# An encoder trunk on one core: the first group's attention heads are split earlier, into the slots of keys that are no longer used

## The chip, the cores and the metric

The kernel runs on one core of a Trainium2 chip. The time is the device time of one execution in microseconds; where one number stands for a kernel it is the median of several executions. The engines are named as in the profile: PE (TensorE, matrix products and transposes), PEld (its weight loads), DVE (VectorE), ACT (ScalarE), POOL (GpSimd) and SP (SyncE, which here only issues DMAs).

## The reference

Two requests, of 512 and 256 tokens, go through two layers with the same weights. All data is float32, the width is 1024.

```python
for i in range(2):
    h = rms_norm(x, norm_mix[i])
    if i == 0:
        x = x + window_attention(h, w_qkv, w_o, sink, band_bias, in_window)
    else:
        x = x + short_conv(h, w_in, conv_w, w_out)
    h = rms_norm(x, norm_mlp[i])
    x = x + square(relu(h @ w_up[i])) @ w_down[i]
    gate = sigmoid(rms_norm(x, norm_ple[i]) @ w_gate[i])
    x = x + (p[i] @ w_proj[i]) * gate
return rms_norm(x, final_norm)
```

The attention has 16 heads of 64 columns in 4 groups; the four heads of a group share one key head and one value head. A query sees the keys that are at most 128 tokens away, a bias for the distance is added, and each head has a learned sink logit that takes part in the softmax's denominator. The heads' outputs go through the output weights `w_o`.

## The kernel before, in words

Everything is held transposed: a tile has 128 columns of the width as partitions and the 768 tokens of both requests side by side. A float32 product is made of three products of rounded parts: each operand is split into a high part, copied by ACT into a rounded type (line 84), and a low part, the rest, subtracted by DVE (line 85). `split` does both. One block of a product is then high × high, high × low and low × high, and a result of 768 tokens is made in two pieces of 512 and 256 tokens that have a bank of PSUM each (`group`, line 140, and `products`). In the attention there is one bank for the 512 piece and one for the 256 piece, so a second result waits until the first has been read out.

The attention (`mixer_attention`) goes over the 4 groups in `attend(g)`, and in each over six blocks of 128 queries, four of the first request and two of the second; a block is called (g, n). A block makes the scores of its four heads on PE (lines 725 and 726; three banks take turns), reduces each with the bias on DVE (line 727), takes exponentials on ACT (747), sums and reciprocals on DVE, scales the probabilities (753, one head on ACT; 755, three on DVE), transposes them on PE (760), splits them (768, 769), multiplies them with the values (770, 771) and writes the sum of both halves into `heads[g]` (773 on ACT, 778 on DVE).

A table `beside` hangs other work behind certain blocks: the queries of later heads (`queries(c)`, 16 heads in 8 pairs), the second half of the keys, the projection of the second layer's extra inputs, and at the end of group 2 the beginning of the output product. `begin_output`, behind block (2, 4), splits the heads of groups 0 and 1 into four tiles each (`aos`; hi parts in slots 16 to 19, lo parts in 24 to 27). `first_output`, behind block (2, 5), loads the first four 128-column blocks of x (`xa`, slots 0 to 3) and adds the products of groups 0 and 1 with `w_o` to them, three matmuls for each of four terms and each of the two pieces, in the order of the list `aos` (lines 793 and 794). `second_output` does the other four with group 2 as well, and `first_head` the rest after the attention.

The slots are 32 tiles of 128 × 768 in SBUF (and ten more later) that are used again and again by number. Slots 0 and 1 hold the doubled high parts of the keys of groups 0 and 1, slots 2 and 3 their low parts; slots 16 to 31 hold the high and low parts of the normalised input, which the query products read to the last pair, behind block (2, 3). A tile given to a used slot waits until the last reader of the one before is done.

Within the attention's loop nobody writes down the order of the instructions: a scheduler orders each engine's instructions when the program is built. It follows the order of the code, and it pulls a later instruction forward where an engine would have nothing to do by its own reckoning and the slots are free. The engines then run their instructions strictly in the order laid down, each waiting for semaphores. SP's queue of DMAs is such an order too.

After the attention, `xs0` and `act0` (lines 1872 and 1873) are lists of slot numbers from which the first layer's MLP takes its places in order, and the last four of `xs0` go to `second_inputs` for the second layer's extra inputs. Later lists are cut out of these two.

Of the kernel before, what the change touches and what calls it, by code (L numbers as in the profile page):

```python
# [11 lines left out]
F32 = mybir.dt.float32  # L12
# [35 lines left out]
def trunk_kernel(ctx: ExitStack, tc: tile.TileContext, a: dict, out: bass.AP):  # L48
# [33 lines left out]
    def split(hi, lo, src):  # L82

        first = act.activation(hi, src, AF.Copy)
        dve.tensor_tensor(lo, src, hi.bitcast(F32), ALU.subtract)
        return first.ins
# [6 lines left out]
    def weight(src, n, raw=None, tag="w"):  # L93

        m = CH if src is None else src.shape[1]
        if raw is None:
            raw = fetch(src)
        pool, bufs = (wp, 2) if tag == "w" else (more, 1)
        hi, lo = (pool.tile([P, CH], F32R, tag=f"{tag}{p}", name=f"{tag}{p}", bufs=bufs) for p in ("hi", "lo"))
        split(hi[:, :m], lo[:, :m], raw[:, :m])  # L100
        return blocks(hi[:, :m], n), blocks(lo[:, :m], n)
# [48 lines left out]
    def slot(i, name, dt=F32R, n=T):  # L150

        return (slots if i < 32 else more).tile([P, n], dt, tag=f"S{i}", name=name)

    def big(name, dt=F32):

        nonlocal turn
        if more is None:
            return tmp.tile([P, T], dt, tag="t", name=name)
        turn += 1
        return tmp.tile([P, T], dt, tag=f"q{turn % 6}", name=name, bufs=1)  # L160

    def terms_of(w, xs, col=0):

        hi, lo = w
        c = slice(col, col + P)
        return [(wh[:, c], wl[:, c], xh, xl) for wh, wl, xh, xl in zip(hi, lo, *xs)]
# [324 lines left out]
    def mixer_attention():  # L491
# [25 lines left out]
        def products(terms):  # L517

            if not split_products:
                ps = psum.tile([P, 1024], F32, tag="mm", name="mm")  # L520
                group(ps, terms)
                yield ps[:, :T], 0, T
                return
            o = 0
            for i, n in enumerate(SEQS):
                ps = psum.tile([P, 512], F32, tag=f"mm{i}", name="mm", bufs=BM)
                group(ps, [(wh, wl, xh[:, o : o + n], xl[:, o : o + n]) for wh, wl, xh, xl in terms], n)
                yield ps[:, :n], o, o + n
                o += n
# [14 lines left out]
        with tc.manual_schedule(engines=order):  # L544
# [21 lines left out]
            hi = wp.tile([P, CH], F32R, name="whi", bufs=2)  # L566
            lo = wp.tile([P, CH], F32R, name="wlo", bufs=2)
# [25 lines left out]
        with s1:  # L593
# [29 lines left out]
            def queries(c):  # L623
                w = wq[0] if c == 0 else weight(a["w_q"][c], KB, raw=wq[1] if c == 1 else None)
                t = big("qt")
                for ps, o, e in products(terms_of(w, xs)):
                    dve.scalar_tensor_tensor(t[:, o:e], ps, HD**-0.5, r[:, o:e], ALU.mult, ALU.mult)
                hi = big("qh", F32R)
                lo = big("ql", F32R)
                split(hi[:], lo[:], t[:])  # L630
                for j in range(2):
                    h = 2 * c + j
                    qst[h] = slot(QS[h % 8], "q")
                    for i, part in enumerate((hi, lo)):
                        nc.sync.dma_start(
                            qst[h][64 * i : 64 * i + 64, :].bitcast(F32),
                            part[64 * j : 64 * j + 64, :].bitcast(F32),
                        )
# [11 lines left out]
            for i, raw in enumerate(rawv):  # L650

                m = min(T, 2 * CH - i * T)
                hi, lo = slot((4, 8, 10)[i], "wvh"), slot((5, 9, 11)[i], "wvl")
# [26 lines left out]
            aos = [], []  # L680
            xa = {}
# [100 lines left out]

            def split_heads(g):
                for i in range(2):
                    hi, lo = (slot(16 + 8 * p + 2 * g + i, "aos") for p in range(2))
                    split(hi[:], lo[:], heads[g][:, i, :])
                    aos[0].append(hi[:])
                    aos[1].append(lo[:])
# [6 lines left out]

            def load_part(m0):
                for m in range(m0, m0 + 4):
                    xa[m] = slot(m, "xa", F32)
                    nc.sync.dma_start(xa[m][:], a["x"][m])

            def first_output():
                load_part(0)
                for j in range(2):
                    w = weight(a["w_o0"][j], 4)
                    for i in range(2):
                        output_part(2 * j + i, w, i * P)

            def second_output():
                split_heads(2)
                load_part(4)  # L810
                for m in range(4, KB):
                    output_part(m, weight(a["w_o1"][m - 4], 6))
# [6 lines left out]
            def projected(n):  # L819
                if n == 0:  # L820
                    projw.append(weight(a["proj"][1, 0], 2))
                for m in range(2 * n, 2 * n + 2):
                    step(1, m, projw[0], part1, "t", False)
# [8 lines left out]
                    for p in range(2):  # L832
                        part1[p].append(ps[p][:, k, :])

            def begin_output():
                for g in range(2):
                    split_heads(g)


            beside = {  # L840
                (0, 5): (inputs1, keys1),
                (1, 4): (lambda: projected(0),),
                (1, 5): (lambda: projected(1),),
                (2, 4): (begin_output,),
                (2, 5): (first_output,),
            }
            for g in range(KV - 1):
                for n in range(2):
                    beside[g, 1 + 2 * n] = (lambda c=2 * g + 2 + n: queries(c),)
            for g in range(KV):  # L850
                attend(g)
            second_output()
            split_heads(3)
        return xa, aos

    xa, aos = mixer_attention()
    psum = ctx.enter_context(tc.tile_pool(name="ps", bufs=8, space=PSUM))
    more = ctx.enter_context(tc.tile_pool(name="more", bufs=1))
# [1010 lines left out]

    xs0 = [*range(32, 42), *range(8, 15), *range(7), *range(16, 20)]
    act0 = [7, *range(20, 24), 28, 29, *range(24, 28), 15, 30, 31]

    rest = xs0[17:] + act0
# [109 lines left out]
```

## Time and profile before

| | |
|---|---|
| timed runs, median (lowest to highest) | 1662.21 us (1659.55 to 1662.38), 3 runs |
| the profiled execution's own time | 1661.51 us |
| its span, first to last instruction | 1659.5 us |
| granted PE clock over the span | 0.996 |
| PE, DVE, ACT busy | 1637.6, 1380.8, 948.5 us |

The profile is of one execution. A row of the timeline has the start in us from the span's start, the duration, the engine, the line, the operation, the tile written and the tiles read, the shape, a count of merged instructions, and in brackets how long the engine stood idle before it and which instruction ended that. Matmuls overlap, so the distance of two starts is the price of one and not its duration. A row of the windows has, for each engine, the busy time in that stretch and the number of instructions.

### The profile page before, as it was taken

How to read it: one execution, taken by the hardware profiler on the slowest of the kernel's cores; microseconds unless marked ns; L12 is line 12 of the kernel's file. 1: busy time of each engine (PE TensorE's matmuls, PEld its weight loads, DVE VectorE, ACT ScalarE, POOL GpSimd, SP SyncE). 2: the span in 40 equal slices, each digit the busy share in tenths (PEclk: the TensorE clock that was granted, in tenths of full speed). 3: DMA queues.
4: the chain of work that ended last, by engine and by line, in shares of the span. 5: the costliest groups of instructions: out<-in, count | busy, mean ns of one | idle time of the engine just before them, and what ended most of it. 6: DMA issues, size and time to landing. Idle time of an engine off the chain costs nothing.

```text
span 1659.5 us, 24297 instructions
## 1 busy us (share of the span) xinstructions
PE 1637.6 (99%) x9414; PEld 1587.3 (96%) x9414; DVE 1380.8 (83%) x2242; ACT 948.5 (57%) x1508; POOL 71.7 (4%) x104
## 2 busy tenths in 40 slices
PE   8999999999999999999999999999999999999997
PEld 7988789999999999999999999999999999999986
DVE  7598888898889889877888777778889888988776
ACT  7377766865556556545654434555555655655554
POOL 0211000000000000000000000000000000000000
PEclk9999999999999999999999999999999999999998
DMA  8755322443233333242312222112333323333222
GB/s 267 199 154 149 87 64 83 121 109 87 83 86 96 96 96 91 71 122 69 98 62 77 76 77 76 64 64 73 87 96 96 95 87 79 90 96 108 69 87 99
DMA packets 55476, 161.11 MB, mean 97 GB/s; under 512 B 7056, under 2 KB 10128, under 8 KB 55360
## 3 DMA queue, kind: packets, MB, share of 16 engines
q1 hardware_dynamic: 45184, 139.89, 26.4%
q0 software_dynamic: 10176, 19.67, 6.7%
q8 instruction: 74, 1.21, 0.3%
q14 instruction: 42, 0.34, 0.1%
HBM read 138.82 MB, written 10.48 MB: 90 GB/s over the span
## 4 chain that ended last, share of the span: by engine, by line
PE 88%; DVE 7%; ACT 4%; issue 1%; DMA 0%; DVEq 0%; SPq 0%; ACTq 0%
PE a L486 33%; PE mm L131 10%; PE mm L140 8%; PE b L486 8%; PE d L486 5%; PE c L486 5%; PE B L486 4%; PE C L486 4%; PE gate L140 3%; PE pt L760 1%; PE p L1096 1%; PE p L1199 1%; PE gate L131 1%; PE O L770 1%; PE O L771 1%
## 5 line engine op out<-in xcount | busy, mean ns | idle before, releaser
L486 PE MATMUL a<-xs,whi 128*128 128x384 f32 x624 | 121.8, 337 | 0.0
L444 ACT ACTIVATE vhi<-wraw 128x512 fp32r<-128x512 f32 x67 | 42.2, 631 | 132.3 <-PE B L486 87.9
L486 PEld LDWEIGHTS a<-xs,whi 128*128 128x128 f32 x624 | 110.0, 188 | 0.2 <-DVE y L1306 0.2
L486 PE MATMUL a<-t,zhi 128*128 128x384 f32 x536 | 109.1, 337 | 0.0
L486 PE MATMUL a<-t,whi 128*128 128x384 f32 x536 | 108.8, 336 | 0.0
L486 PE MATMUL b<-t,zhi 128*128 128x384 f32 x536 | 108.7, 336 | 0.0
L1341 DVE TENSOR_TENSOR x<-x,a 128x384 f32<-128x384 f32 x112 | 62.1, 554 | 55.3 <-PE a L486 55.3
L486 PE MATMUL a<-act,whi 128*128 128x384 f32 x448 | 96.5, 337 | 0.0
L486 PEld LDWEIGHTS a<-t,whi 128*128 128x128 f32 x536 | 94.9, 188 | 0.0
L486 PEld LDWEIGHTS b<-t,zhi 128*128 128x128 f32 x536 | 94.9, 188 | 0.0
L486 PEld LDWEIGHTS a<-t,zhi 128*128 128x128 f32 x536 | 94.8, 188 | 0.0
L464 DVE TENSOR_TENSOR wlo<-wraw,whi 128x1024 fp32r<-128x1024 f32 x70 | 85.2, 1218 | 7.9 <-ACT whi L444 7.9
L444 ACT ACTIVATE whi<-sum 128x1024 fp32r<-128x1024 f32 x67 | 70.6, 1054 | 27.0 <-PE a L486 22.7
L464 DVE TENSOR_TENSOR wlo<-sum,whi 128x1024 fp32r<-128x1024 f32 x67 | 81.8, 1220 | 5.1 <-ACT whi L444 5.1
L1058 ACT ACTIVATE y<-y 128x768 f32<-128x768 f32 x64 | 53.7, 839 | 54.4 <-DVE y L1055 54.3
L464 DVE TENSOR_TENSOR zlo<-sum,zhi 128x1024 fp32r<-128x1024 f32 x67 | 81.5, 1217 | 0.0
L140 PE MATMUL mm<-xs_mix,whi 128*128 128x512 f32 (+1 forms) x320 | 81.0, 341 | 0.0
L486 PEld LDWEIGHTS a<-act,whi 128*128 128x128 f32 x448 | 79.8, 188 | 0.0
L444 ACT ACTIVATE whi<-wraw 128x1024 fp32r<-128x1024 f32 x72 | 75.7, 1051 | 7.0 <-PE C L486 7.0
L444 ACT ACTIVATE zhi<-sum 128x1024 fp32r<-128x1024 f32 x67 | 70.9, 1058 | 11.9 <-DVE sum L420 11.0
L486 PE MATMUL a<-xs,wlo 128*128 128x384 f32 x312 | 67.1, 336 | 0.0
L358 ACT ACTIVATE t<-y 128x768 fp32r<-128x768 f32 x56 | 45.7, 838 | 34.9 <-DVE y L349 34.4
(345 smaller groups left out, 4558.4 us busy)
## 6 DMA issues: line engine op xcount, KB each, us to landing
wraw<-in_up SPq DMA_DIRECT2D x64, 512.0 KB, 3.9
wraw<-in_down SPq DMA_DIRECT2D x64, 512.0 KB, 4.2
wraw<-in_w_in SPq DMA_DIRECT2D x24, 512.0 KB, 3.5
wraw<-in_gate SPq DMA_DIRECT2D x16, 512.0 KB, 3.4
vlo<-in_up POOLq DMA_DIRECT2D x28, 256.0 KB, 5.6
vlo<-in_down POOLq DMA_DIRECT2D x28, 256.0 KB, 6.0
pj<-pjs SPq DMA_DIRECT2D x16, 384.0 KB, 2.8
wraw<-in_w_q SPq DMA_DIRECT2D x8, 512.0 KB, 4.6
```

Of the source, the lines that this page charges most:

```text
L131: pe.matmul(t, lhsT=w, rhs=x[:, o:e], start=first and i == 0 and j == 0, stop=last and i == n - 1 and j == 2)
L140: pe.matmul(ps[:, o:e], lhsT=w, rhs=x[:, o:e], start=i == 0 and j == 0, stop=i == n - 1 and j == 2,)
L358: act.activation(t[0][:], (self.q1, self.q2)[i][:], AF.Copy)
L444: act.activation(hi[:], src, AF.Copy)
L464: dve.tensor_tensor(lo[:], src, hi[:].bitcast(F32), ALU.subtract)
L486: pe.matmul(ps, lhsT=a, rhs=b, start=start and i == 0, stop=i == len(terms) - 1, skip_group_check=True)
L760: pe.transpose(pt[:, h * P : (h + 1) * P], lg[h // 2][:, h % 2, b * P : (b + 1) * P], ident[:],)
L770: pe.matmul(O[:], lhsT=v, rhs=ph[:], start=b == 0, stop=False)
L771: pe.matmul(O[:], lhsT=v, rhs=pl[:], start=False, stop=b == nk - 1)
L1058: act.activation(t[:], t[:], AF.Square)
L1096: pe.matmul(ps[o], lhsT=wt[:, c], rhs=xs[f"x{h + 1}{1 + o}"][m][part], start=k == 0 and j == 0, stop=k == KB - 1 and j == 2,)
L1341: dve.tensor_tensor(t[:, o : o + H], t[:, o : o + H], f, op)
```

## The change

The split of group 0's heads is hung behind block (2, 1) instead of (2, 4), and its four tiles go into slots 0 to 3 (hi in 0 and 1, lo in 2 and 3), whose keys are not read after group 1. The split of group 1 stays behind (2, 4). The first four `xa` tiles go into slots 24, 25, 16 and 17 instead of 0 to 3. In `xs0`, slots 0 to 3 move to the end, where the second layer's extra inputs take their places, and 16 to 19 move ahead of them.

```diff
             def split_heads(g):
                 for i in range(2):
-                    hi, lo = (slot(16 + 8 * p + 2 * g + i, "aos") for p in range(2))
+                    hi, lo = (slot(2 * p + i if g == 0 else 16 + 8 * p + 2 * g + i, "aos") for p in range(2))
...
                 for m in range(m0, m0 + 4):
-                    xa[m] = slot(m, "xa", F32)
+                    xa[m] = slot((24, 25, 16, 17, 4, 5, 6, 7)[m], "xa", F32)
                     nc.sync.dma_start(xa[m][:], a["x"][m])
...
-            def begin_output():
-                for g in range(2):
-                    split_heads(g)
...
-                (2, 4): (begin_output,),
+                (2, 4): (lambda: split_heads(1),),
...
+            beside[2, 1] += (lambda: split_heads(0),)
...
-    xs0 = [*range(32, 42), *range(8, 15), *range(7), *range(16, 20)]
+    xs0 = [*range(32, 42), *range(8, 15), *range(4, 7), *range(16, 20), *range(4)]
```

What the scheduler makes of it is seen in the order of the instructions. The first place is DVE at the end of group 2, about 197 to 207 us in the profile of before. `aos` of heads_772 is group 0, of heads_1400 group 1; the numbers behind L, S and O tell buffers apart. Before:

```order
L727 ISA L_2450,mx_2440<-S_2455,bias_1406,sink_77 128x256
L727 ISA mx_2440 128x1
L778 TENSOR_TENSOR heads_2021<-O_2344,ot_2367 64x2x128 x2
L740 TENSOR_SCALAR nm_2459<-mx_2440 128x4
L742 TENSOR_TENSOR es_2461<-sink_77,mx_2440 128x4
L85 TENSOR_TENSOR aos_2507<-heads_772,aos_2506 128x768
L85 TENSOR_TENSOR aos_2511<-heads_1400,aos_2510 128x768
L85 TENSOR_TENSOR aos_2515<-heads_1400,aos_2514 128x768
L748 TENSOR_TENSOR sm_2464<-sm_2464,es_2461 128x4
L727 ISA L_2519,mx_2518<-S_2520,bias_1401,sink_77 128x256
```

And in the changed kernel:

```order
L727 ISA L_2458,mx_2448<-S_2463,bias_1406,sink_77 128x256
L727 ISA mx_2448 128x1
L85 TENSOR_TENSOR aos_2515<-heads_1400,aos_2514 128x768
L778 TENSOR_TENSOR heads_2021<-O_2352,ot_2375 64x2x128 x2
L740 TENSOR_SCALAR nm_2467<-mx_2448 128x4
L742 TENSOR_TENSOR es_2469<-sink_77,mx_2448 128x4
L727 ISA L_2519,mx_2518<-S_2520,bias_1401,sink_77 128x256
L727 ISA mx_2518 128x1
L727 ISA L_2519,mx_2518<-S_2524,bias_1401,sink_77 128x256
```

The three subtractions in one piece are one here, the last of group 1 (its first stands some rows earlier), and the reductions of the next block follow directly.

The second place is PE at the same time. In the changed kernel this stands there, where `mm_2594` and `mm_2608` are the two pieces of the first output block, `aos_2515` the last split of group 1, `mm_2622` the first piece of the second output block, which has the same bank as `mm_2594`:

```order
L140 MATMUL mm_2594<-aos_2515,whi_2590 128x512
L140 MATMUL mm_2594<-aos_2514,wlo_2591 128x512
L140 MATMUL mm_2608<-aos_2515,whi_2590 128x256
L140 MATMUL mm_2608<-aos_2514,wlo_2591 128x256
L725 MATMUL S_2533<-khh_1388,q_1816 128x256
L726 MATMUL S_2533<-kll_1389,q_1816 128x256
L725 MATMUL S_2715<-khh_1394,q_2230 128x256
L726 MATMUL S_2715<-kll_1395,q_2230 128x256
L725 MATMUL S_2719<-khh_1394,q_2233 128x256
L726 MATMUL S_2719<-kll_1395,q_2233 128x256
L725 MATMUL S_2724<-khh_1394,q_2442 128x256
L726 MATMUL S_2724<-kll_1395,q_2442 128x256
```

The next row is the first matmul of `mm_2622`. Before, the last three of these score pairs stood behind the first output block's products with the transposes between, and the order there was this, with `aos_2507` the second split (the low part) of group 0:

```order
L725 MATMUL S_2520<-khh_1388,q_1609 128x256
L726 MATMUL S_2520<-kll_1389,q_1609 128x256
L725 MATMUL S_2524<-khh_1388,q_1612 128x256
L726 MATMUL S_2524<-kll_1389,q_1612 128x256
L725 MATMUL S_2529<-khh_1388,q_1813 128x256
L726 MATMUL S_2529<-kll_1389,q_1813 128x256
L140 MATMUL mm_2594<-aos_2507,whi_2590 128x512
```

The third place is DVE near 169 us, in group 2's first blocks, as a piece of the difference:

```order
-L85 TENSOR_TENSOR wlo<-wraw,whi 128x1024
-L748 TENSOR_TENSOR sm<-sm,es 128x4
-L740 TENSOR_SCALAR nm<-mx 128x4
-L742 TENSOR_TENSOR es<-sink,mx 128x4
-L749 RECIPROCAL sm<-sm 128x4
+L85 TENSOR_TENSOR aos<-heads,aos 128x768
+L748 TENSOR_TENSOR sm<-sm,es 128x4
+L740 TENSOR_SCALAR nm<-mx 128x4
+L742 TENSOR_TENSOR es<-sink,mx 128x4
+L749 RECIPROCAL sm<-sm 128x4
+L85 TENSOR_TENSOR wlo<-wraw,whi 128x1024
 L755 TENSOR_SCALAR L<-L,sm 128x256 x3
```

The second subtraction of group 0 takes the place of that of a query weight, which moves behind the reciprocal and ahead of the scalings. The first one stands near 127 us, behind three scalings; the two copies of ACT stand near 123 and 162 us. On SP the loads of `xa` 0 to 3, which were issued at 108 and 156 us, stand together behind the q loads of the seventh pair of heads and a load of `w_o`, and ahead of the q loads of the eighth pair. From the end of the attention on, the order on every engine is as it was.

## Prediction

> **What bounds the kernel now.** I read the page first: busy shares, then the chain that ended last.
>
> ```profile
> PE 1637.6 (99%) x9414; PEld 1587.3 (96%) x9414; DVE 1380.8 (83%) x2242; ACT 948.5 (57%) x1508; POOL 71.7 (4%) x104
> ...
> PE 88%; DVE 7%; ACT 4%; issue 1%; DMA 0%; DVEq 0%; SPq 0%; ACTq 0%
> ```
>
> TensorE (PE) is the bound nearly everywhere, so an edit pays only where PE stands still or is slow. The next view is the busy time by stretches of 10 us, then of 1 us, around the change. Columns are PE, PEld, DVE, ACT, POOL busy, then the granted clock, the DMA share and GB/s.
>
> ```profile
> 200.00:210.00 10.00, 8.44 (x43) 7.08 (x42) 8.76 (x28) 4.27 (x14) 0.00 (x0) 0.83 0.47 158
> ```
> ```profile
> 201.00:202.00 1.00, 0.00 (x0) 0.00 (x0) 0.97 (x4) 0.47 (x2) 0.00 (x0) 1.00 0.66 169
> 202.00:203.00 1.00, 0.52 (x1) 0.50 (x2) 1.00 (x2) 1.00 (x6) 0.00 (x0) 0.62 1.05 399
> 203.00:204.00 1.00, 1.00 (x4) 0.73 (x3) 1.00 (x2) 0.70 (x4) 0.00 (x0) 0.50 0.55 218
> ```
>
> This is the poorest stretch of the attention stage: PE does nothing from 201 to 202 while DVE is full, and then the granted clock falls to half. The waits of PE in 100 to 420 us name the cause, and PE's timeline shows it:
>
> ```profile
> PE mm L140 <- DVE aos L85: 1.6, 1, 1.6
> ```
> ```profile
> 200.65 0.28 PE L726 MATMUL S<-kll,q 128*128 128x256 f32 x1
> 202.48 0.79 PE L140 MATMUL mm<-aos,whi 128*128 128x512 f32 x1 [1.56 <-DVE aos L85]
> ...
> 204.35 0.63 PE L140 MATMUL mm<-aos,whi 128*128 128x512 f32 x1
> 204.78 0.63 PE L140 MATMUL mm<-aos,wlo 128*128 128x512 f32 x1
> ...
> 206.93 1.03 PE L760 MATMUL pt<-ident,L 128*128 128x128 f32 x8
> 207.72 0.36 PE L140 MATMUL mm<-aos,wlo 128*128 128x256 f32 x1
> ...
> 212.36 0.39 PE L140 MATMUL mm<-aos,wlo 128*128 128x512 f32 x1
> 212.59 0.40 PE L140 MATMUL mm<-aos,whi 128*128 128x256 f32 x2
> 212.83 0.28 PE L140 MATMUL mm<-aos,wlo 128*128 128x256 f32 x1
> ```
>
> The starts give the price of a matmul: 0.23 us for 512 columns (212.36 to 212.59), 0.12 for 256 (two in 212.59 to 212.83), and 0.43 for 512 at half clock (204.35 to 204.78). PE waits for the low parts of the split heads (line 85). DVE is the engine in front:
>
> ```profile
> 196.52 0.48 DVE L727 CUSTOM_DVE_ANT_0 L<-S,bias,sink 128x256 f32<-128x256 f32 x1
> ...
> 197.87 1.29 DVE L769 TENSOR_TENSOR pl<-pt,ph 128x512 fp32r<-128x512 f32 x2
> ...
> 199.08 0.47 DVE L727 CUSTOM_DVE_ANT_0 L<-S,bias,sink 128x256 f32<-128x256 f32 x1
> ...
> 199.48 0.48 DVE L727 CUSTOM_DVE_ANT_0 L<-S,bias,sink 128x256 f32<-128x256 f32 x1
> ...
> 200.45 0.85 DVE L778 TENSOR_TENSOR heads<-O,ot 64x256 f32<-64x256 f32 x2
> ...
> 201.47 2.69 DVE L85 TENSOR_TENSOR aos<-heads,aos 128x768 fp32r<-128x768 f32 x3
> ...
> 204.08 0.16 DVE L748 TENSOR_TENSOR sm<-sm,es 128x4 f32<-128x4 f32 x1
> ...
> 205.02 0.87 DVE L755 TENSOR_SCALAR L<-L,sm 128x256 f32<-128x256 f32 x3
> ...
> 207.19 0.68 DVE L794 TENSOR_TENSOR xa<-xa,mm 128x512 f32<-128x512 f32 x1
> ...
> 209.86 0.41 DVE L794 TENSOR_TENSOR xa<-xa,mm 128x256 f32<-128x256 f32 x1
> ```
>
> Three splits stand in one block at 201.47 (0.88 us each by their pitch, and a fourth ran at 193.3). One of those three is of group 0, and PE's first products need it.
>
> **The change part by part.**
>
> *The split of group 0 moves.* Two ACT copies and two DVE subtractions leave the stretch from 192 to 204 us. What DVE then does I chain row by row from 196.52, where nothing before it has moved. Two score reductions at a pitch of 0.40 (199.08 to 199.48) end at 197.3. The two heads additions (0.85) need ACT's ot, so ACT's rows come first:
>
> ```profile
> 194.78 0.84 ACT L84 ACTIVATE qh<-qt 128x768 fp32r<-128x768 f32 x1
> ...
> 198.69 1.06 ACT L84 ACTIVATE whi<-wraw 128x1024 fp32r<-128x1024 f32 x1
> 199.82 0.60 ACT L773 ACTIVATE ot<-O 64x512 f32<-64x512 f32 x1
> ...
> 201.53 0.51 ACT L747 ACTIVATE L<-L,nm 128x256 f32<-128x256 f32 x1 [1.11 <-DVE nm L740]
> ```
>
> After qh (to 195.6) now come whi (1.06) and ot (0.60), to 197.2: in time. So heads end at 198.2, the two pl (1.2) at 199.4, two more reductions (0.8) at 200.2, the last split of group 1 (0.88) at 201.1, heads (0.85) at 201.95, nm and es at 202.1, four reductions (1.6) at 203.7, and the 512-column addition to xa (0.68) at 204.4. Then sm, nm, es and the reciprocal (four small ones, 0.45), the 256-column xa (0.33 by its pitch in a row of others, 0.41 at most) and three scalings (0.87) end at about 206.1.
>
> PE, in its new order, first runs six 512-column products of group 0 with no wait, and has done the whole first output chunk (twelve of 512, twelve of 256) but its last products, which need the split that ends at 201.1. Those (two of 512, two of 256) run from 201.1 to 201.9. Next in PE's order are four score pairs (0.24 each), each waiting for one of the four reductions that run from 202.1 to 203.7, and behind them the second chunk's products, which wait for the xa addition at 204.4. **So a new lull replaces the old one**: from 201.9 to 204.4 PE has 1.0 us of work. Then five 512-column products (1.2) to 205.6, and the transposes wait for the scalings and end near 206.7.
>
> The balance at that mark, the end of these eight transposes: before at 207.72 with twelve 512s and eleven 256s of aos; after at about 206.7 with seventeen and twelve, and three more score pairs. That is 1.0 us of time, plus 5 × 0.235 + 7 × 0.117 = 2.0 us of work already done: **−3.0 us**. DVE is ahead by the same measure (two xa additions, two reductions, 1.9 us), so the lead isn't handed back at the next block. The half clock, about 1.5 us of the old stretch, is inside this balance and not added again; I take it that it doesn't come back, as the new lull is cut into pieces under 1 us by the score pairs.
>
> *Where the split now stands.* The scheduler puts the pieces still earlier than the code does, at four places, here with the idle time that each meets:
>
> ```profile
> 123.00 0.51 ACT L747 ACTIVATE L<-L,nm 128x256 f32<-128x256 f32 x1 [1.11 <-DVE nm L740]
> ...
> 163.01 0.59 ACT L773 ACTIVATE ot<-O 64x512 f32<-64x512 f32 x1 [1.04 <-PE O L771]
> ```
> ```profile
> 128.70 0.42 DVE L627 SCALAR_TENSOR_TENSOR qt<-mm,rstd_mix 128x256 f32<-128x256 f32 x1 [1.25 <-PE mm L140]
> ...
> 168.97 1.22 DVE L85 TENSOR_TENSOR wlo<-wraw,whi 128x1024 fp32r<-128x1024 f32 x1
> ...
> 170.53 0.88 DVE L755 TENSOR_SCALAR L<-L,sm 128x256 f32<-128x256 f32 x3
> 173.14 0.69 DVE L627 SCALAR_TENSOR_TENSOR qt<-mm,rstd_mix 128x512 f32<-128x512 f32 x1 [1.73 <-PE mm L140]
> ```
> ```profile
> 171.54 1.09 PE L760 MATMUL pt<-ident,L 128*128 128x128 f32 x8
> ```
>
> In the first fence ACT, in the second DVE, in the third the PE row that the last two bear on. Three fit into idle time of 1.0 to 1.25 us (0.84 on ACT, 0.95 on DVE): free; without that cover each would cost its own length. The fourth, on DVE, takes wlo's place at 168.97, and wlo (1.22) now stands ahead of the scalings, which end at 172.2 and not 171.4. The transposes at 171.54 read them; PE's order has only one product moved between, so I count 0.5 us of wait, of which half comes back, as the wait for ph behind them goes: **+0.25** (bounds 0 and 0.8).
>
> *The loads of xa 0 to 3* move on SP from 108 and 156 us to behind the release of the slots by the last query product, near 189, ahead of four q loads. They are wanted at 203.7. I take **0**, bounds 0 and the slower rival below.
>
> *The places of the second layer's input parts*: the same sequence of tiles with other slots. The instructions and their waits behind the attention stand as they did; slots 0 to 3 are last read by the output products, as 16 to 19 were. **0**; were one of them late, the split that writes it would wait on ACT, which idles 43% of the span.
>
> Sum: −3.0 + 0.25 = −2.75 us, on the profiled execution's 1661.51 (its span of 1659.5 and 2 around it): 1658.8. That execution is 0.7 under the median of the three timed runs, so in their terms it would be 1659.5; I put the forecast between, at 1659.2. A measurement here can tell about 0.2% from no change, 3.3 us.
>
> [...]
>
> **The rivals.**
>
> *More is won (−4 to −5).* If reductions, scalings and xa come to PE's needs earlier than in my chain (it takes DVE's rows one after the other at full length), there is no new lull of note, and PE loses nothing from 197 to 207. For it: PE's gaps outside this stretch are small. Against: DVE is 100% busy in 201 to 204, and only 1.8 us leave it. Time 1657.2.
>
> *The clock falls again.* The old fall came after idle times in pieces too, and the new lull holds 1.0 us of work in 2.5. Then about 1.5 us of the gain are lost: 1660.9.
>
> *The q loads come late: slower.* SP is one queue; four xa loads now wait ahead of the q loads of heads 14 and 15, and the fourth of the new score pairs needs them at 203.7, with all filler products behind it on PE.
>
> ```profile
> 195.64 0.46 SPq L635 DMA_DIRECT2D q<-qh  x1
> ```
> ```profile
> DMA to landing us min/median/max: 3.1/3.7/6.9
> ```
> ```profile
> 198.00:199.00 1.00, 0.84 (x3) 0.44 (x3) 1.00 (x2) 1.00 (x3) 0.00 (x0) 1.00 0.98 249
> ```
>
> The first row is the issue of the first q load, the second the xa loads' time to landing, the third a stretch with the DMA engines full. If a load of 384 KB takes 3.5 us (two that shared the engines took 6.9) and all are served one after the other, four end 14 us after 189, and four q loads of half the size 7 us later, at 210. The fourth score pair then starts 6.3 us late and PE stands still for that: less the gain of 2.75, 3.5 us slower, 1665.0. It decides the sign from a landing after 206.5 on. Against it: at 249 GB/s the four loads (1.57 MB) need 6.3 us and are done at 195.3, before the first q load is issued.
>
> **How the numbers follow.** The sum as worked out 0.56, more 0.22, the clock again 0.15, slower 0.07. The range of 1657.0 to 1661.8 takes in the sum with its bounds and the clock's second fall; it leaves out the slower rival and the lower half of "more". Faster by over 0.2% is all of "more" and the part of the first case in which its bounds add up well (0.16): 0.38. Slower by over 0.2%: 0.06. Within: 0.56.
>
> **What would show each step right or wrong.** In the changed kernel PE should not wait for aos before its second output chunk; its wait should be for mx (line 727, a score bank) and then for xa (line 794), about 1.5 us together, some 2 us after the place of the old one. The granted clock should read 1.00 in all slices near 200. The eight transposes that now end at 207.7 should end near 207, with more aos products ahead of them, and those at 171.54 some 0.5 us later. The xa loads should be issued near 189 and land by 196, and no score pair should wait for q. It would be wrong if PE's wait at the transposes of 171.54 spread to the blocks behind, if the sum of PE's pauses from 196 to 215 came out as in the kernel before, or if the clock fell at another place.

## The result and the profile after

| series | before, median | changed, median | ratio, 95% interval |
|---|---|---|---|
| first | 1661.63 us (16 runs) | 1658.19 us (16) | 0.9983, 0.9976 to 0.9989 |
| second (e1) | 1660.19 us (33) | 1657.52 us (11) | 0.9978, 0.9969 to 0.9987 |
| third (c1) | 1661.54 us (23) | 1658.04 us (11) | 0.9983, 0.9974 to 0.9993 |

The changed kernel is faster by about 0.2%, at the edge of what the prediction called measurable; the forecast was 1659.2. Three executions of changed kernels took 5067, 2295 and 2002 us with PE slowed (busy for 5049.8 us in the first, a mean granted clock of 0.66 and 0.75 in the others); they are left out of the ranges and means below, though not of the medians, and as the first of them was the profiled one, the profile after is that of the second series. The profiled execution there took 1657.51 us, against the 1661.51 of before's. The rows that answer to those of before begin with the page and the stretches; the columns are the same.

```profile
PE 1635.5 (99%) x9414; PEld 1585.3 (96%) x9414; DVE 1380.6 (83%) x2242; ACT 948.4 (57%) x1508; POOL 71.7 (4%) x104
...
PE 89%; DVE 7%; ACT 3%; issue 1%; DMA 0%; DVEq 0%; SPq 0%; ACTq 0%
```
```profile
200.00:210.00 10.00, 9.34 (x52) 7.21 (x51) 9.72 (x34) 6.88 (x23) 0.00 (x0) 1.00 0.64 199
```
```profile
201.00:202.00 1.00, 0.91 (x4) 0.68 (x4) 0.96 (x6) 0.00 (x0) 0.00 (x0) 1.00 0.68 197
202.00:203.00 1.00, 0.54 (x4) 0.38 (x3) 1.00 (x6) 0.97 (x4) 0.00 (x0) 1.00 0.76 255
203.00:204.00 1.00, 1.00 (x7) 0.79 (x6) 1.00 (x5) 1.00 (x5) 0.00 (x0) 1.00 0.43 114
```

PE has 52 matmuls in 200 to 210 us, where it had 43, and the clock stays at 1.00. The empty microsecond from 201 to 202 is gone; DVE is as full as it was. PE's timeline shows what stands there instead:

```profile
200.71 0.28 PE L726 MATMUL S<-kll,q 128*128 128x256 f32 x1
201.09 0.50 PE L140 MATMUL mm<-aos,whi 128*128 128x512 f32 x1
...
201.77 0.28 PE L140 MATMUL mm<-aos,wlo 128*128 128x256 f32 x1
202.51 0.39 PE L725 MATMUL S<-khh,q 128*128 128x256 f32 x1 [0.46 <-DVE mx L727]
...
203.95 0.28 PE L726 MATMUL S<-kll,q 128*128 128x256 f32 x1
204.33 0.74 PE L140 MATMUL mm<-aos,whi 128*128 128x512 f32 x2
...
205.60 1.06 PE L760 MATMUL pt<-ident,L 128*128 128x128 f32 x8
206.42 0.48 PE L140 MATMUL mm<-aos,wlo 128*128 128x512 f32 x1
```

The wait for `aos` is 0.26 us (200.71 plus a price of 0.12, to 201.09). From 201.89 to 204.33 PE does eight score matmuls, 0.94 us of work in 2.44: this is the new lull, with its wait on mx in front and the xa addition at its end. The eight transposes end at 206.42, and the trace has 17 products of 512 columns and 12 of 256 from `aos` ahead of that mark. DVE's rows are the chain that PE follows:

```profile
197.19 0.84 DVE L778 TENSOR_TENSOR heads<-O,ot 64x256 f32<-64x256 f32 x2
198.06 1.29 DVE L769 TENSOR_TENSOR pl<-pt,ph 128x512 fp32r<-128x512 f32 x2
...
200.07 0.96 DVE L85 TENSOR_TENSOR aos<-heads,aos 128x768 fp32r<-128x768 f32 x1
200.94 0.85 DVE L778 TENSOR_TENSOR heads<-O,ot 64x256 f32<-64x256 f32 x2
...
203.18 0.48 DVE L727 CUSTOM_DVE_ANT_0 L<-S,bias,sink 128x256 f32<-128x256 f32 x1
...
203.59 0.69 DVE L794 TENSOR_TENSOR xa<-xa,mm 128x512 f32<-128x512 f32 x1
...
204.85 0.88 DVE L755 TENSOR_SCALAR L<-L,sm 128x256 f32<-128x256 f32 x3
205.63 1.22 DVE L85 TENSOR_TENSOR wlo<-wraw,whi 128x1024 fp32r<-128x1024 f32 x1
```

### The profile page after: what moved, and what is told of

Its sections match the earlier page's. It is cut to its first block, busy times and chain, and to the rows that moved or that the text cites. A ratio compares the mean times of both kernels' runs of the same rounds, so it can differ in the third digit from the quotient of the medians.

```text
span 5065.1 us, 24305 instructions
## 1 busy us (share of the span) xinstructions
PE 5049.8 (100%) x9414; PEld 3700.1 (73%) x9414; DVE 1413.3 (28%) x2242; ACT 966.3 (19%) x1508; POOL 71.5 (1%) x104
## 4 chain that ended last, share of the span: by engine, by line
PE 100%; DMA 0%; DVE 0%; ACT 0%; issue 0%; DVEq 0%; SPq 0%; ACTq 0%
PE a L486 34%; PE mm L140 11%; PE mm L131 9%; PE b L486 8%; PE c L486 5%; PE d L486 5%; PE gate L131 5%; PE B L486 4%; PE C L486 4%; PE gate L140 3%; PE p L1093 2%; PE p L1196 2%; PE pt L760 2%; PE c L1768 1%; PE S L725 1%; PE S L726 1%
## 5 line engine op out<-in xcount | busy, mean ns | idle before, releaser
L486 PE MATMUL a<-xs,whi 128*128 128x384 f32 x624 | 350.8, 786 | 0.0
L486 PE MATMUL a<-t,zhi 128*128 128x384 f32 x536 | 309.5, 784 | 0.0
L486 PE MATMUL b<-t,zhi 128*128 128x384 f32 x536 | 309.2, 786 | 0.0
L486 PE MATMUL a<-t,whi 128*128 128x384 f32 x536 | 309.2, 786 | 0.0
L486 PE MATMUL a<-act,whi 128*128 128x384 f32 x448 | 267.0, 787 | 0.0
L486 PE MATMUL d<-t,vhi 128*128 128x384 f32 x312 | 176.7, 786 | 0.0
L486 PE MATMUL c<-xs,whi 128*128 128x384 f32 x312 | 176.0, 786 | 0.0
L131 PE MATMUL gate<-xs_ple,whi 128*128 128x384 f32 x256 | 175.2, 889 | 0.0
L486 PE MATMUL a<-t,zlo 128*128 128x384 f32 x268 | 167.1, 791 | 0.0
L486 PE MATMUL b<-t,zlo 128*128 128x384 f32 x268 | 166.8, 786 | 0.0
```

The costliest lines, as they stand in the source:

```text
L131: pe.matmul(t, lhsT=w, rhs=x[:, o:e], start=first and i == 0 and j == 0, stop=last and i == n - 1 and j == 2)
L486: pe.matmul(ps, lhsT=a, rhs=b, start=start and i == 0, stop=i == len(terms) - 1, skip_group_check=True)
```

## Where the time went

PE's order has 9414 matmuls in each kernel. The first 600 are the same in all, and from the 2400th on they do the same work in the same order, so the time from the 600th (near 105 us) to the 2400th (near 417 us) is the price of the attention, and that from the 2400th to the 9400th the price of what follows. These are distances of two starts, taken from the trace of each profile in us:

| profile | matmul 600 starts | 600 to 2400 | 2400 to 9400 | clock near 200 us |
|---|---|---|---|---|
| before | 104.79 | 314.40 | 1225.37 | falls |
| b2, before again | 105.24 | 314.55 | 1225.36 | falls |
| b1, before again | 104.14 | 313.07 | 1225.37 | 1.00 |
| e1, changed | 104.51 | 311.31 | 1224.83 | 1.00 |
| c1, changed | 105.37 | 311.40 | 1224.81 | 1.00 |
| e2, hook only | 105.07 | 312.08 | 1225.42 | 1.00 |
| e3, slots only | 104.48 | 311.29 | 1224.84 | 1.00 |
| e4, two more subtractions | 104.60 | 314.24 | 1224.79 | falls |
| e6, one more | 104.63 | 313.53 | 1224.84 | falls |
| e5, both groups early | 105.12 | 310.17 | 1224.81 | 1.00 |
| c2, both groups early | 104.14 | 310.46 | 1224.79 | 1.00 |
| e7, other places for xa | 104.53 | 310.24 | 1224.85 | 1.00 |
| f1, list reversed | 105.18 | 311.38 | 1224.77 | 1.00 |

Two profiles of one kernel differ by 0.3 us at most in the third column (b1 apart) and by 0.02 in the fourth. From the first profile of before to e1 the time falls by 4.0 us: 3.09 in the attention, 0.54 behind it, 0.28 at the start, the rest at the end and outside the span. The start is no doing of the change: it differs as much between profiles of one kernel.

## The experiments

The theory was the prediction's: DVE's queue at the end of group 2 holds PE up, and the change pays by taking 1.8 us of DVE work out of it, with the clock as an extra. The rivals: that the place in the code or the six products of group 0 without a wait are what counts, and that the new lull drops the clock again.

**e1, the changed kernel once more.** No edit.

> The changed kernel itself, for a profile and more times. If DVE's queue at the end of group 2 was the cause (the theory of the prediction): the eight transposes that ended at 207.7 us end at 206.7, with PE's wait on aos (1.56 us) gone and about 1.5 us of waits on line 727 and line 794 in 202 to 204.5; the granted clock is 1.00 from 195 to 215; the transposes of 171.5 end 0.5 us later; 2.5 to 3 us under the kernel before. If the new lull drops the clock again: 0.5 in one stretch near 204 to 208 and only 1 to 1.5 us under it.

The rows above are its profile. The theory's numbers came out: transposes to 206.42 instead of 206.7, no fall of the clock, 2.7 us between the medians, and 1.5 us of pauses in the lull. Two points did not: PE still waits 0.26 us for `aos`, and the transposes of 171.5 are not half a microsecond later (below).

**e2, the hook alone.** Before, with the split of group 0 behind (2, 1), but in the old places:

```diff
-                (2, 4): (begin_output,),
+                (2, 4): (lambda: split_heads(1),),
...
+            beside[2, 1] += (lambda: split_heads(0),)
```

> The kernel before with the split of group 0 hung behind (2, 1) but with its old places 16, 17, 24 and 25, which the query products read until about 189 us, and the old lists. If what matters is that the places are free: the split still runs behind 189 us, DVE is as full from 196 to 206 as before, and the time is within 0.5 us of the kernel before. If the place in the code alone matters: the split runs ahead of 190 us and 2 us or more of the gain is there.

1659.19 us, 0.9990 (0.9981 to 0.9999) of the kernel before: neither answer. DVE's rows show why; both subtractions of group 0 run as soon as the places are free, 190.3 us, and the last one of group 1 still at 201.45:

```profile
190.32 1.82 DVE L85 TENSOR_TENSOR aos<-heads,aos 128x768 fp32r<-128x768 f32 x2
...
201.45 0.95 DVE L85 TENSOR_TENSOR aos<-heads,aos 128x768 fp32r<-128x768 f32 x1
```
```profile
PE S L725 <- DVE mx L727: 0.5, 1, 0.5
PE mm L140 <- DVE aos L85: 0.5, 1, 0.5
```

The second fence is of PE's waits: one pause of 1.6 us became two of 0.5. I had not thought of the queue from 190 to 196 us as having room. Of the 1.76 us that the change saves in the attention beside the clock (313.07 to 311.31; b1 is the one profile of before without a fall), this alone gives 0.99, and none of its 11 executions took over 1659.89 us; the free places give the rest.

**e3, the places alone.** The changed kernel with the split of group 0 behind (2, 4) again:

```diff
-                (2, 4): (lambda: split_heads(1),),
+                (2, 4): (lambda: split_heads(0), lambda: split_heads(1)),
...
-            beside[2, 1] += (lambda: split_heads(0),)
```

> The changed kernel with the split of group 0 hung behind (2, 4) again, just ahead of that of group 1, its places 0 to 3 and the other lists kept. If free places are what lets the split go forward: it stands ahead of 190 us and the time is within 0.6 us of the changed kernel. If the hook is needed: DVE has its subtractions in 192 to 204 us again, PE waits for aos, and the time is within 0.6 us of the kernel before.

1658.21 us, 0.9984 (0.9975 to 0.9993), and 311.29 in the table: the changed kernel again, though the median is 0.7 over e1's, a little more than the 0.6 expected (the means are 0.5 apart), and the orders near 170 us are not quite the same. The tile's group has the starts of the four subtractions, and they are those of the changed kernel (127.2 to 200.1):

```profile
L85 DVE TENSOR_TENSOR aos<-heads,aos x4: 928/956/958, 127.1 to 200.0; 128x768 fp32r<-128x768 f32 x4
```

With free places the scheduler pulls the split forward by itself. The hook alone brings part of the gain; the places alone bring all of it.

**e4 and e6, the DVE work put back.** The changed kernel with two subtractions, or one, of the same size behind the split of group 1, into a tile that nobody reads. `again` follows in the list behind (2, 4); e6 has `range(1)`:

```diff
+            def again():
+                for i in range(2):
+                    dum = ap.tile([P, T], F32, name="dum", bufs=1)
+                    dve.tensor_tensor(dum[:], heads[1][:, i, :], aos[0][2 + i].bitcast(F32), ALU.subtract)
```

> The changed kernel with two more subtractions of 128x768 on DVE behind those of group 1, whose results nobody reads; this puts 1.8 us of DVE work back into the stretch from 196 to 206 us, while the products of group 0 stay free of it. If DVE's length there is what PE pays for: 1.5 to 2.5 us slower than the changed kernel, more if the clock falls there again. If the gain came from the six products of group 0 that wait for nothing: at most 0.7 us slower than the changed kernel.

> The changed kernel with one more subtraction of 128x768 on DVE behind those of group 1, whose result nobody reads: half the dose of the one with two. If DVE's length in the stretch is the price: 0.9 us slower than the changed kernel without a fall of the clock, 0.9 and about 2 more in executions where it falls; between 1658.4 and 1660.8 in all, with two groups of times if the fall depends on where the lull meets the clock's windows. If the products of group 0 were what counted: within 0.4 us of the changed kernel.

e4 took 1660.85 us (1.0002, 0.9993 to 1.0011), 3.3 over the changed kernel of the same series; e6 1659.86 (0.9996, 0.9987 to 1.0005), about 2 over the changed kernel's medians. All of e4's eleven executions lie from 1660.07 to 1662.03; of e6's ten, nine lie from 1658.98 to 1660.30 and one at 1657.48, whose mean granted clock is 0.998 where the others have 0.996 or 0.997. The traces show that the clock stays at half for 3.41 us in each of the four profiles with a fall near 200 us; whether the lull's place decides a fall, as the second expectation supposes, is not shown. PE's waits of e4, then of e6, and the stretch behind the lull of each, where the clock is the number after POOL:

```profile
PE S L725 <- DVE mx L727: 2.1, 2, 1.3
```
```profile
PE S L725 <- DVE mx L727: 1.5, 2, 1.3
```
```profile
205.11:208.52 3.41, 3.41 (x15) 3.25 (x15) 3.41 (x12) 1.91 (x5) 0.00 (x0) 0.50 0.57 210
```
```profile
205.23:208.64 3.41, 3.23 (x14) 2.70 (x13) 2.88 (x9) 1.74 (x5) 0.00 (x0) 0.50 0.54 199
```

Nothing that PE reads waits for the added work; it stands in DVE's queue ahead of reductions, in e4 as `dum`:

```profile
201.98 0.95 DVE L839 TENSOR_TENSOR dum<-heads,aos 128x768 f32<-128x768 f32 x1
202.85 0.48 DVE L727 CUSTOM_DVE_ANT_0 L<-S,bias,sink 128x256 f32<-128x256 f32 x1
...
203.25 0.95 DVE L839 TENSOR_TENSOR dum<-heads,aos 128x768 f32<-128x768 f32 x1
```

PE's wait on mx grows from 0.5 to 1.5 and 2.1 us, and the clock falls. So DVE's length is the price, and the products of group 0 without a wait don't protect PE. The table has it: 311.31, 313.53 with one subtraction, 314.24 with two, where the kernel before has 314.40; the fall is in all of these but the first. The scheduler also lays the orders behind the added work anew: in e6 a few products near the 1200th matmul and the additions to xa change places, in e4 PE's order differs up to the 1509th matmul. So the sum of e4 is not the price of its two subtractions alone, while the waits on mx come straight from them.

**b1 and b2, the kernel before, for its clock.** No edit. Of 77 timed runs of it in three series (beside e1, b1 and c1), 42 lie at 1658.80 to 1660.30 (mean 1659.56) and 35 at 1661.36 to 1663.12 (mean 1662.02), with none between; the 16 of the first series lie in the same two ranges, 7 and 9.

> The kernel before once more, for its profile. Its times fall in two groups, 1659.2 to 1660.2 and 1661.6 to 1662.8 us. If these are executions without and with the fall of the clock behind PE's pause: a time in the lower group comes with a clock of 1.00 in all of 200 to 210 us and the same pause on aos of 1.5 us, one in the upper group with 3.4 us at 0.5. If the groups have another cause, the clock falls in either.

> The same once more, so that both groups are likely to be seen: expectations as for the first.

One of each came: b1 took 1659.38 us, b2 1661.91. PE's rows have the same pause in both, b1 first:

```profile
201.89 0.50 PE L140 MATMUL mm<-aos,whi 128*128 128x512 f32 x1 [1.55 <-DVE aos L85]
```
```profile
202.94 0.50 PE L140 MATMUL mm<-aos,whi 128*128 128x512 f32 x1 [1.55 <-DVE aos L85]
```
```profile
200.47:203.88 3.41, 1.99 (x11) 1.73 (x12) 3.38 (x8) 2.17 (x9) 0.00 (x0) 1.00 0.71 231
203.88:207.29 3.41, 3.41 (x26) 3.06 (x25) 3.41 (x15) 1.60 (x3) 0.00 (x0) 1.00 0.48 135
```
```profile
199.93:203.34 3.41, 1.86 (x9) 1.25 (x9) 3.30 (x12) 2.23 (x8) 0.00 (x0) 1.00 0.69 200
203.34:206.75 3.41, 3.41 (x12) 2.83 (x11) 3.41 (x13) 1.33 (x5) 0.00 (x0) 0.50 0.19 77
```

The last two fences are the stretches of 3.41 us with the pause and behind it, of b1 and of b2. With the same wait the clock stays in one and falls in the other, for 3.413 us, at a price of 1.3 to 1.5 us in the table's third column. The two groups of times are executions without and with that fall: the mean granted clock of the 77, too, is 0.997 or more in all 42 of the lower group and 0.996 in 33 of the 35 of the upper (0.997 in two).

**e5, both groups early.** This was to beat the changed kernel: group 1 is split behind (2, 1) too, its parts in the places of heads 0 and 3, and heads 3 in that of heads 1:

```diff
-                heads[g] = pair(g, "heads")
+                heads[g] = pair((0, 1, 2, 1)[g], "heads")
...
+                if g == 1:
+                    ps = [pair(3 * p, "aos", F32R) for p in range(2)]
                 for i in range(2):
+                    if g == 1:
+                        hi, lo = (t[:, i, :] for t in ps)
...
-                (2, 4): (lambda: split_heads(1),),
...
-            beside[2, 1] += (lambda: split_heads(0),)
+            beside[2, 1] += (lambda: split_heads(0), lambda: split_heads(1))
```

> The changed kernel with the split of group 1 hung behind (2, 1) as well: its hi and lo parts go into the places of heads 0 and of heads 3, and heads 3 takes that of heads 1. This takes the two subtractions of 193.2 and 200.1 us, 1.8 us of DVE, out of the stretch too. If DVE's length there is still the price: the lull from 201.8 to 204.3 shrinks by 1 to 1.5 us, and the time is 0.7 to 1.5 us under the changed kernel. If DVE has no room left in 150 to 190 us: the subtractions delay scalings and transposes there, PE waits at several places, and the time is within 0.5 us of the changed kernel or above it.

> The kernel with both groups split early once more, beside the changed kernel on one chip. If the gain of DVE's length goes on: 0.7 to 1.2 us under the changed kernel, intervals apart from no difference. If the first measurement owed it to the clock's start: within 0.3 us.

> The changed kernel once more, on the chip of the next two: 1657.5 us, without a fall of the clock between 100 and 1600 us.

1656.60 us in its first series (0.9975, 0.9966 to 0.9984). Beside the changed kernel on one chip (c2 and c1) it took 1656.26 us against 1658.04, 0.9972 (0.9962 to 0.9983) of before against 0.9983. The mean of its 7 runs there is 1.67 us lower (resampling the runs gives a ratio of 0.9987 to 0.9993), more than the 0.7 to 1.2 expected. The third column has 0.8 to 1.2 us of it and the fourth nothing; the rest may be the start, which moves from execution to execution, but this is not shown. All four subtractions now end before 176 us (group of the tile, then PE's waits, both of c2):

```profile
L85 DVE TENSOR_TENSOR aos<-heads,aos x4: 951/953/958, 126.8 to 175.0; 128x768 fp32r<-128x768 f32 x4
```
```profile
PE pt L760 <- ACT L L753: 0.6, 1, 0.6
PE S L725 <- DVE es L742: 0.5, 1, 0.5
PE b L486 <- DVE zlo L464: 0.4, 1, 0.4
```

The first (near 159 us) and the third (behind 250) are in the kernel before too. From 197 to 212 only the second is left, for `es`. In e5's first profile a wait of 0.31 us stood in its place, for the load of q at 203.64, and SP's rows show why: the fifth xa load held the queue until its place was free.

```profile
189.35 8.17 SPq L804 DMA_DIRECT2D xa<-in_x  x5
198.26 1.11 SPq L635 DMA_DIRECT2D q<-qh  x2
```

**e7, other places for xa.** e5 with `(24, 25, 16, 17, 18, 19, 26, 27)[m]` for the xa tiles.

> Both groups split early, and the last four xa tiles in the places 18, 19, 26 and 27, which that leaves free, instead of 4 to 7. There PE waited 0.31 us for the load of q, which stood on SP behind an xa load that waited 6.0 us for its place. If that place is the cause: q is issued near 196 us, PE's wait on it goes, and it is 0.2 to 0.3 us under the kernel with both groups early. If four more xa loads in the DMA queues delay q as much: no gain, or a longer wait for q and up to 1 us more.

1656.72 us (0.9976, 0.9968 to 0.9985), and 310.24: no gain. The q loads are issued 0.6 us sooner, not at 196:

```profile
188.79 3.84 SPq L804 DMA_DIRECT2D xa<-in_x  x7
197.71 0.47 SPq L635 DMA_DIRECT2D q<-qh  x1
```

PE no longer waits for q, but for the addition to xa, 0.26 us. What was won at one wait was lost at the next.

**f1, the list reversed.** The last eight places of `xs0` as 19 to 16 and 3 to 0.

> The changed kernel with the last eight places of the list in reverse order. In every kernel with the new list the matmuls from 420 to 1640 us take 0.5 to 0.6 us less than in the kernel before, and with the old list they do not. If the numbers of the places decide it (where a tile lies): another order moves this sum by 0.2 us or more. If it is what the new list shares with this one, that 0 to 3 come last: again 0.5 to 0.6 us less than in the kernel before. The attention is as in the changed kernel in either case.

1657.83 us in a single run; the fourth column has 1224.77, like all kernels with the new list (1224.77 to 1224.85), where the old one has 1225.36 to 1225.42. It isn't the order within the eight. No matmul gains 0.1 us from before to e1 there; the half microsecond is made of steps of a few ns over 7000 matmuls. What makes it was not found.

## Why the prediction was right

*The chain.* It held row by row. Expected ends and the changed kernel's (by the start of the next row): heads 198.2 and 198.1, pl 199.4 and 199.3, the last split 201.1 and 200.9, heads 201.95 and 201.8, reductions 203.7 and 203.6, the xa addition 204.4 and 204.3, scalings 206.1 and 205.6. The lull was to be 201.9 to 204.4 with 1.0 us of work; it is 201.9 to 204.3 with 0.94. The 17 and 12 products ahead of the mark are the forecast's. By its 600th matmul this profile is 0.28 us ahead of the one that the chain was drawn from, so the two agree to 0.2 us either way. One sign was wrong: PE was not to wait for `aos` ahead of the second output block, and waits 0.26 us.

*The balance.* −3.0 expected; by the same measure 207.72 − 206.42 is 1.30, and 1.99 of work, −3.3, or −3.0 without the 0.28 of the start. The table has −3.1 for the whole attention, from a profile in which the clock fell.

*The fourth early piece* was to cost 0.25. It cost 0.14 for about 2 us and nothing in the end:

```profile
168.83 0.95 DVE L85 TENSOR_TENSOR aos<-heads,aos 128x768 fp32r<-128x768 f32 x1
...
170.00 1.20 DVE L85 TENSOR_TENSOR wlo<-wraw,whi 128x1024 fp32r<-128x1024 f32 x1
171.12 0.88 DVE L755 TENSOR_SCALAR L<-L,sm 128x256 f32<-128x256 f32 x3
```
```profile
171.13 0.82 PE L760 MATMUL pt<-ident,L 128*128 128x128 f32 x4
171.71 0.48 PE L140 MATMUL mm<-xs_mix,whi 128*128 128x512 f32 x1
172.03 0.60 PE L760 MATMUL pt<-ident,L 128*128 128x128 f32 x4
172.38 0.48 PE L140 MATMUL mm<-xs_mix,whi 128*128 128x512 f32 x1
```

The scalings do run 0.6 us later (171.12, before 170.53), but PE takes the eight transposes in two halves with the moved product between, the first of them on ACT's head. It comes to them 0.14 us ahead of the kernel before (the product ahead of them starts at 170.90, there at 171.04) and is level at the next product, at 172.38 in both. By the 1002nd matmul, near 174 us, the 0.14 is made up. I had counted the wait and not the part of it that the order already covers.

*The xa loads* went out at 188.36 (expected near 189), PE waits for no q, and the price was 0:

```profile
188.36 2.26 SPq L799 DMA_DIRECT2D xa<-in_x  x4
...
195.50 0.47 SPq L635 DMA_DIRECT2D q<-qh  x1
```

A q load held up on SP behind an xa load is seen in e5 alone, by a place that was not yet free, and it cost 0.31 us there and not 6.

*The clock* is where the prediction was right with a wrong idea. It took the fall as part of the kernel before, 1.5 us inside the balance, and held the new lull to be safe because score pairs cut it into pieces. The size is right (1.3 to 1.5), but the fall comes in only 35 of 77 executions, and whether the pause is cut does not tell the cases apart: b1's is one piece of 1.55 us and its clock stays, e4's is cut into 1.33 and 0.77 us by a score pair and its clock falls. The gain is therefore two numbers. Against an execution with the fall, it is 3.1 in the attention and 0.5 behind it; against one without, 1.76 and 0.54. By the means, the changed kernel's 21 runs of the second and third series have 1657.8, which is 4.2 under the upper group and 1.75 under the lower. The groups differ by 2.5 us and not by 1.4, as the start differs too: the 600th matmul starts 0.65 and 1.1 us later in the two profiles of before with the fall than in b1.

The clock records show where the starts part. The clock turns full 9.31 us after the span's start in b1, 11.09 in before and 12.20 in b2 (PE goes there from 5 matmuls in a microsecond to 7). In these three the fall comes with the two later starts; why is not shown. Over the 13 profiles the 600th matmul follows this instant closely, from 104.14 at 9.31 to 105.37 at 12.26. The median of before moves between 1659.8 and 1662.2 with the share of falls, and I set the forecast against one end of it.

*How near the number came* is in part luck. In the mean, before and changed are 2.9 us apart (1660.7 over the 77 runs, 1657.8 over the 21). An estimate from the table puts it together as 1.76 of DVE's queue, 0.55 of the places list and 0.6 of the fall (1.4 in 35 of 77). The forecast's 2.75 has the whole fall and nothing of the list.

*The clock's second fall* (0.15) shows in none of the changed kernel's 36 executions (a mean granted clock of 0.997 or 0.998 in each), but it was near: one subtraction more brings it (e6).

*The places list* was put at 0, and 0.55 us came with it, by a way that stays open.

## What to carry to other kernels

When an engine off the critical path is full for a stretch, what counts is how much stands in its queue there, whoever reads it: 0.95 us of work that nobody waits for cost PE 2.2, the fall of the clock and a slightly other order included. Work with early inputs should be given a place to be written to early; a scheduler that may pull forward then does the rest, and where the places are held, moving the code alone gave 1.0 us of the 1.8. A kernel whose times come in two groups is best taken apart by profiles of both, before a median is chosen to forecast against.

## What the runs showed of the hardware that was not expected

The clock fell near 200 us behind lulls that were not empty: matmuls filled 0.20 to 0.35 of the last 3.41 us ahead of it. In the first profile of before the clock records are at half for 3.413 us from 202.241 and again from 1649.492 to the end, with the rows

```profile
1646.08:1649.49 3.41, 1.19 (x4) 0.59 (x4) 2.39 (x8) 2.40 (x4) 0.00 (x0) 1.00 0.20 77
1649.49:1652.90 3.41, 0.68 (x2) 0.01 (x1) 2.64 (x6) 1.30 (x3) 0.00 (x0) 0.50 0.25 94
```

on either side of the second instant. In the four profiles with a fall near 200 us, the matmuls, at their prices in the trace (0.234 us for 512 columns, 0.117 for 256, 0.109 for 128), filled this much:

| profile | 3.41 us ahead of the fall | share filled | clock in the next 3.41 us |
|---|---|---|---|
| e4 | 201.70 to 205.11 | 0.20 | 0.50 |
| b2 | 199.93 to 203.34 | 0.29 | 0.50 |
| e6 | 201.82 to 205.23 | 0.31 | 0.50 |
| before | 198.83 to 202.24 | 0.35 | 0.50 |

In e1, whose clock stays at 1.00, the 3.41 us from 201.89 with the new lull were filled to 0.53, and the emptiest 3.41 us between 200 and 207.5 to 0.48. How little PE did does not settle it, though. An estimate: b1 starts its first product at 201.89 and before at 202.48, and by before's rows, 0.59 us earlier, the 3.41 us ahead of that product are filled to about 0.31 in b1 too, yet its clock stays at 1.00. Nor does the longest idle time: it is 1.3 us in e6, where the clock falls, and 1.55 in b1, where it stays. What sets b1 apart from b2 was not shown.
